# A hybrid decoder layer on one core: attention scores from split operands, x in three tiles that W_out fills, y split two tiles ahead, and other orders at two places

## The chip, the cores and the metric

The kernel runs on 1 core of one Trainium2 chip. The metric is the device time of one execution in microseconds (us). Engines are named as in the profile: PE (TensorE matmul), PEld (TensorE weight load), DVE (VectorE), ACT (ScalarE), POOL (GpSimd), SP (SyncE, which issues the DMAs).

## The reference, cut to what matters

One layer on 1024 tokens of width 1024, with 16 meta tokens ahead of them, so 1040 positions:

```
xn   = rms_norm(h)                                   # h: 1040 x 1024
z, xbc, dt, q, k, v = split(xn @ w_in)               # q, k, v: 16 heads of 64
y_ssd = ssd_mixer(z, xbc, dt, ...)                   # Mamba-2, chunks of 128
zlog = (q_t . k_s) / 8                               # per head
A[t,s] = sigmoid(zlog[t,s]) * prod_{s<j<t} (1 - sigmoid(zlog[t,j]))     # s < t
y_sb = rms_norm(A @ v)
h    = h + rms_norm([y_ssd ; y_sb] @ w_out)
g, u = split(rms_norm(h) @ w_up)                     # 2816 columns each
h    = h + rms_norm((gelu(causal_dwconv3(g)) * u) @ w_down)
```

Everything is float32, and the output is the last 1024 rows of h.

## The kernel before, in words

Large products are taken in float32r (F32R in the code, fp32r in the profile). An operand a is split into a_hi, its copy in float32r (an ACT copy), and a_lo = a - a_hi (a subtract on DVE or POOL), and a product is the sum of three matmuls, hi·hi + hi·lo + lo·hi, in one PSUM bank. Smaller products (scores, the mix with the values, transposes) are plain float32; the trace has two records for each such matmul of the scores.

**Projections.** The normed x stands transposed in two tiles, `xh` and `xl` (128 x 8 x 1040). `project_steps` (L154) makes 128 output columns of `w_in`: for each token third of `CH` (348, 346, 346 tokens) and each of 8 blocks of the contraction three matmuls (L162, `pj_*`), 24 in a third; ACT evacuates it. The projections for the attention are generators that other code advances by one step; a step is a third, or with `halves_` half a third (12 matmuls). They are the *fill* of the attention.

**Decays.** At 70 to 90 us the mixer's dt goes through a chain of small DVE operations (up to `s` and `adh`, L522 and L526), then `decays` (L531) multiplies it by three triangular matrices (`pz_ea`, `pz_de`, `pz_cd`) and ACT takes exponentials. Before it four steps of projections (`run(fill, 4)`) and the transposes of B (`bc[0][1][0]`, tiles `tt_B`) are issued.

**Attention.** A loop over 8 pairs of heads p and 8 query blocks i (L898). The order on PE is written out by hand (`manual_schedule`, L896): PE does what stands next in the code. For block i:

- `block_weights` (L682): scores `z` (L699) of 128 queries against n = 16 + 128(i+1) keys, in chunks of at most 512 keys (one chunk for i up to 2, two for i from 3 to 6, three for i = 7). The two heads of the pair lie on rows 0 to 63 and 64 to 127 of q and k. ACT makes two sigmoids of each chunk (`kp` L700, `bt` L701); DVE scans `kp` along the keys (L704) and POOL multiplies `bt` by it (L706), once per head.
- fill: one or two half steps of projections between the scores and what follows.
- `block_mix` (L725): `av` (L734), the product with the values, of the block whose transposes stand one block earlier.
- `block_turn` (L709): `tw` (L720), the transposes of `bt` of the block two earlier; ACT copies them to `th` (L722).
- one more half step of fill.

z and tw share two PSUM buffers ("zz"). In pair 6 the projections end; the x tiles are freed, and the first half of `w_out` is loaded, split into `woha`/`wola` (L827, L828) and multiplied with two halo rows (`halo`, L820), all behind blocks 5 and 6. From then on the fill is the first half of the output product, `ssd_half` (L876): for each token tile t, `split_y` loads `yk` and splits it into `yh` (ACT, L859) and `yl` (POOL, L860), and `out_steps` makes two halves of 24 matmuls (`mo`, L870). In pair 7 a half is placed only behind blocks 1, 3, 5, 6 and 7; `split_y` for tile t+1 stands ahead of the product of tile t.

**After the attention** the second half of `w_out` is loaded (`wor`, `worb`) and split, with its halo matmuls, while `ssd_half` ends with tiles 6 to 8. Then the second product runs tile by tile; `ev2` (L1322) adds it to the first, `after` (L1011 to L1024) takes the norms, `turn_x2` (L1030) transposes, and the feed-forward part begins with the products `g0a` and `u0a` (L1180). Their weights are split into `wh` (ACT, L1108) and `wl` (POOL, L1109). From t = 6 on the order on PE, DVE, ACT and POOL is that of the code (L1312).

Of the kernel before, what the change touches and what calls it, by code (L numbers as in the profile page):

```python
# [8 lines left out]
F32 = mybir.dt.float32  # L9
# [22 lines left out]
CH = [(0, 348), (348, 346), (694, 346)]  # L32
# [19 lines left out]
def tile_layer(ctx: ExitStack, tc: tile.TileContext, x, meta, rows, parts,  # L52
# [101 lines left out]
    def project_steps(w, ncol, xh, xl, chunks, evac, name, halves_=False):  # L154
        hi, lo = w
        for c0, n in chunks:
            acc = psum_mm(f"pj_{name}_{c0}")
            for k in range(KB):
                if halves_ and k == KB // 2:
                    yield  # L160
                for j, (a, b) in enumerate(((hi, xh), (hi, xl), (lo, xh))):
                    mm(acc[:ncol, :n], a[:, k, :ncol], b[:, k, c0:c0 + n],  # L162
                       start=(k == 0 and j == 0), stop=(k == KB - 1 and j == 2))
# [33 lines left out]
    xh = xp.tile([P, KB, L], F32R, name="xh", tag="xh")  # L197
    xl = xp.tile([P, KB, L], F32R, name="xl", tag="xl")

    def conv_chain(b, nm, w, halves_=False):  # L200
# [5 lines left out]

        return raw, project_steps(w, P, xh, xl, CH, ev, nm, halves_)

    dtT = rp.tile([32, L + 3], F32, name="dtT", tag="rt", bufs=1)

    def dt_steps(hl):
        for c0, n in CH:
            acc = psum_mm(f"pj_dt_{c0}")
            for k in range(KB):
                for j, src in enumerate((xh, xl)):
                    mm(acc[:32, :n], hl[:, k, :], src[:, k, c0:c0 + n],
                       start=(k == 0 and j == 0), stop=(k == KB - 1 and j == 1))
# [4 lines left out]
    with tc.tile_pool(name="pre", bufs=3, side="right") as pre, \  # L222
# [46 lines left out]
        def turn_x(i):  # L269
            c0, nr = spans[i]  # L270
            tps = []
            for hf in range(2):
# [6 lines left out]
                tps.append((tp, (slice(None), slice(4 * hf, 4 * hf + 4), slice(c0, c0 + nr))))  # L279
            for tp, dst in tps:  # L280
                nc.scalar.activation(xh[dst], tp[:, :, :nr], AF.Copy)
            for tp, dst in tps:
                nc.vector.tensor_tensor(xl[dst], tp[:, :, :nr], xh[dst].bitcast(F32), op=ALU.subtract)
# [62 lines left out]
    def qkv_block(name, evac, halves_):  # L346
        w = weights_of(name)
        for i, _ in enumerate(project_steps(w, P, xh, xl, CH, evac, name, halves_)):
# [3 lines left out]

    def qkv_steps(p, post):
        q = rp.tile([P, L + 3], F32, tag="rq", name=f"q{p}", bufs=3)
        k = rp.tile([P, L], F32, tag="rk", name=f"k{p}", bufs=3)
        for dst, nm in ((q, "q"), (k, "k")):
            def ev(acc, c0, n, dst=dst):
                nc.scalar.activation(dst[:, c0:c0 + n], acc[:, :n], AF.Copy)

            yield from qkv_block(f"{nm}{p}", ev, p > 1 or (p, nm) == (1, "k"))  # L360
        vt = rp.tile([P, L], F32, tag="rt", name=f"vt{p}", bufs=1)

        def evv(acc, c0, n):
            nc.scalar.activation(vt[:, c0:c0 + n], acc[:, :n], AF.Copy)

        v = rp.tile([P, NT + 1, P], F32, tag="rv", name=f"v{p}")
        vc = rp.tile([P, P], F32, tag="vc", name=f"vc{p}")
        heads[p] = q, k, v, vc
        yield from qkv_block(f"v{p}", evv, p > 0)

        def turn_v(part):
            tp = psum_tp(f"vtp{p}_{part}")
# [5 lines left out]
        def turn_edge():  # L378
            edge = rp.tile([P, NT, NM], F32, tag="edge", name=f"edge{p}", bufs=1)
# [7 lines left out]
            nc.vector.tensor_copy(meta_k[:, p, :], k[:, 0:NM])  # L387
# [20 lines left out]
    with tc.tile_pool(name="ssd", bufs=1, side="right") as sp:  # L408
# [49 lines left out]
        def z_steps(g, b):  # L458
# [5 lines left out]
            yield from project_steps(load_w(w_z[4 * g + b], P, f"z{g}{b}"), P, xh, xl, CH, evz, f"z{g}{b}")  # L464
# [75 lines left out]
        run(fill, 4)  # L540
        bc[0][1][0]()
        decays()
        tmp.close()
        run(fill)

# [135 lines left out]

    def block_weights(p, i):  # L682
        q, k = heads[p][:2]
        nm = f"{p}_{i}"
        if i == 0:
            edges[p] = ap.tile([P, 2, NT, NM], F32, tag="cb", name=f"cb{p}", bufs=2)
            nc.gpsimd.memset(edges[p][:, :, :, NM - 1:], 0.0)
        t0, n = NM + i * P, NM + (i + 1) * P
# [4 lines left out]
        for ci, (a, w) in enumerate(chunks):  # L693
# [3 lines left out]
            for j in range(2):  # L697
                h = halves[j]
                mm(z[:, j, :w], q[h, t0:t0 + P], k[h, a:a + w], start=True, stop=True)  # L699
            nc.scalar.activation(kp[:, :, a:a + w], z[:, :, :w], AF.Sigmoid, scale=-QSCALE)  # L700
            nc.scalar.activation(bt[:, :, a:a + w], z[:, :, :w], AF.Sigmoid, scale=QSCALE)  # L701
        m = n - NM
# [1041 lines left out]
```

## Time and profile before

| what | value |
|---|---|
| median of 3 runs | 1810.53 us (1805.03 to 1811.18) |
| the profiled execution | 1805.86 us |
| its span in the profile | 1804.2 us (1.66 us lie around it) |
| mean granted TensorE clock | 0.989 |
| busy | PE 1732.4 us (96%), PEld 1487.3, DVE 1061.6, ACT 830.8, POOL 867.8 |

Start of pairs: the first score of pair 0 is at 415.2 us and that of pair 7 at 880.5; the last scores are at 940.8. The page gives busy time by engine; the windows give it by stage; the timeline shows each instruction's start with the idle time ahead of it and what ended that. A line such as `L820` is a line of the kernel before.

### The profile page before, as it was taken

To read this page: it belongs to the slowest core of one execution; us is meant where nothing else is said; L and a number is where in the kernel's file an instruction comes from. 1 tells how busy PE (TensorE), PEld (TensorE's weight loads), DVE (VectorE), ACT (ScalarE), POOL (GpSimd) and SP (SyncE) were. 2 spreads that over 40 slices of the span, in tenths; PEclk is the share of its full clock that TensorE was granted. 3 is DMA by queue.
4 is the path that set the end of the run, shared out by engine and by line. 5 is a ranking of instruction groups with operands and counts; after the bars stand their busy time and mean duration, and the time that the engine had idled before them with its cause. 6 is when DMAs were issued, how large, how long until landed. Compare 5 with 4: busy or idle time off the path is not lost. (4 is left out here: it accounts for less than half of the span.)

```text
span 1804.2 us, 27314 instructions
## 1 busy us (share of the span) xinstructions
PE 1732.4 (96%) x10942; PEld 1487.3 (82%) x10942; DVE 1061.6 (59%) x1125; ACT 830.8 (46%) x1373; POOL 867.8 (48%) x615
## 2 busy tenths in 40 slices
PE   6999999999999999999799899899999999999997
PEld 6899889888888888886567588888999988888886
DVE  5651964873463454355741256666766666657988
ACT  5423553645565565566653333543333333244444
POOL 4223753676555564554751223277777776600001
PEclk9999999999999999999999899999999999999999
DMA  4133333231011011012212545222333332196344
GB/s 157 48 97 106 106 118 107 71 94 36 24 37 48 24 36 37 24 48 71 72 42 95 193 140 164 82 88 88 117 100 106 101 105 88 64 320 227 95 123 158
DMA packets 90547, 173.96 MB, mean 96 GB/s; under 512 B 10698, under 2 KB 35818, under 8 KB 90420
## 3 DMA queue, kind: packets, MB, share of 16 engines
q1 hardware_dynamic: 90420, 172.21, 30.0%
q8 instruction: 86, 1.41, 0.3%
q14 instruction: 41, 0.34, 0.1%
HBM read 122.39 MB, written 49.79 MB: 95 GB/s over the span
## 5 line engine op out<-in xcount | busy, mean ns | idle before, releaser
L704 DVE TENSOR_TENSOR_SCAN kp<-kp,hold 128x272 f32<-128x272 f32 (+7 forms) x128 | 207.8, 1665 | 193.5 <-ACT kp L700 103.2
L706 POOL TENSOR_TENSOR bt<-bt,kp 128x256 f32<-128x256 f32 (+7 forms) x128 | 214.7, 1695 | 188.9 <-DVE kp L704 132.7
L1109 POOL TENSOR_TENSOR wl<-wr,wh 128x1024 fp32r<-128x1024 f32 x44 | 110.7, 2524 | 40.7 <-ACT wh L1108 40.7
L1557 PE MATMUL dn<-dl,dh 128*128 128x512 f32 x308 | 119.9, 389 | 0.1
L1557 PE MATMUL dn<-dh 128*128 128x512 f32 x308 | 119.9, 389 | 0.0
L1557 PE MATMUL dn<-dh,dl 128*128 128x512 f32 x308 | 119.8, 389 | 0.0
L1603 POOL TENSOR_TENSOR fms<-fms,nhalf 128x1 f32<-128x1 f32 x8 | 8.5, 1060 | 225.7 <-DMA ar<-fda 186.0
L700 ACT ACTIVATE kp<-z 128x288 f32<-128x288 f32 (+6 forms) x112 | 82.8, 739 | 56.7 <-PE z L699 33.0
L1486 ACT ACTIVATE dh<-ar 128x512 fp32r<-128x512 f32 x77 | 48.7, 632 | 111.3 <-PE dn L1557 90.7
L699 PE MATMUL z<-k,q 64*128 64x144 f32 (+6 forms) x448 | 86.9, 487 | 13.3 <-ACT bt L701 6.0
L1108 ACT ACTIVATE wh<-wr 128x1024 fp32r<-128x1024 f32 x44 | 46.6, 1060 | 114.7 <-PE fX L1166 68.3
L1238 DVE SCALAR_TENSOR_TENSOR ga<-gr,pp,ga 128x1024 f32<-128x1024 f32 x44 | 71.4, 1622 | 34.8 <-ACT ga L1231 34.0
L722 ACT ACTIVATE th<-tw 128x1024 f32<-128x1024 f32 (+2 forms) x96 | 74.7, 813 | 34.1 <-PE tw L720 32.2
L701 ACT ACTIVATE bt<-z 128x288 f32<-128x288 f32 (+6 forms) x112 | 83.1, 742 | 0.0
L720 PE MATMUL tw<-ident,bt 128*128 128x128 f32 x576 | 77.6, 280 | 3.8 <-issue 2.8
L734 PEld LDWEIGHTS av<-th,v 128*64 128x64 f32 x1152 | 62.6, 138 | 18.9 <-issue 17.9
L734 PE MATMUL av<-th,v 128*64 128x128 f32 x1152 | 78.0, 281 | 0.0
L1487 DVE TENSOR_TENSOR dl<-ar,dh 128x512 fp32r<-128x512 f32 x77 | 53.2, 691 | 41.7 <-ACT dh L1486 41.7
L720 PEld LDWEIGHTS tw<-ident,bt 128*128 128x128 f32 x576 | 62.1, 141 | 15.5 <-issue 12.9
L699 PEld LDWEIGHTS z<-k,q 64*128 64x128 f32 x448 | 36.7, 186 | 41.8 <-issue 18.5
L1557 PEld LDWEIGHTS dn<-dl,dh 128*128 128x128 f32 x308 | 57.8, 188 | 12.5 <-DVE dl L1487 0.4
L1557 PEld LDWEIGHTS dn<-dh 128*128 128x128 f32 x308 | 57.8, 188 | 12.4 <-ACT dh L1486 0.3
(550 smaller groups left out, 5752.6 us busy)
## 6 DMA issues: line engine op xcount, KB each, us to landing
wr<-in_w_up SPq DMA_DIRECT2D x44, 512.0 KB
fds<-ga SPq DMA_DIRECT2D x44, 256.0 KB
b<-in_w_down SPq DMA_DIRECT2D x44, 256.0 KB
ar<-fds SPq DMA_DIRECT2D x44, 256.0 KB
fda<-ga SPq DMA_DIRECT2D x33, 256.0 KB
ar<-fda SPq DMA_DIRECT2D x33, 256.0 KB
yk<-yd SPq DMA_DIRECT2D x16, 512.0 KB
zd<-zt SPq DMA_DIRECT2D x8, 520.0 KB
```

The lines of the kernel that those rows point to most:

```text
L699: mm(z[:, j, :w], q[h, t0:t0 + P], k[h, a:a + w], start=True, stop=True)
L700: nc.scalar.activation(kp[:, :, a:a + w], z[:, :, :w], AF.Sigmoid, scale=-QSCALE)
L701: nc.scalar.activation(bt[:, :, a:a + w], z[:, :, :w], AF.Sigmoid, scale=QSCALE)
L704: nc.vector.tensor_tensor_scan(kp[:, j][:, ::-1], kp[:, j][:, ::-1], hold[:, L - n:L][:, ::-1], 0.0, op0=ALU.mult, op1=ALU.max)
L706: nc.gpsimd.tensor_tensor(bt[:, j, 0:m], bt[:, j, 0:m], kp[:, j, 1:m + 1], op=ALU.mult)
L720: nc.tensor.transpose(tw[:, j, b, :], bt[:, j, c0:c0 + P], ident)
L722: nc.scalar.activation(th[:, :, :nb, :], tw[:, :, :nb, :], AF.Copy)
L734: mm(av[halves[j], :], v[:, kb, halves[j]], th[:, j, b, :], start=kb == 0, stop=kb == i)
L1109: nc.gpsimd.tensor_tensor(l, raw, h.bitcast(F32), op=ALU.subtract)
L1238: nc.vector.scalar_tensor_tensor(v, self.g[jj][:, :, i:i + 256], fconv_w[:, j, i:i + 1], v, op0=ALU.mult, op1=ALU.add)
L1487: sub(lo[:, k], raw, hi[:, k].bitcast(F32), op=ALU.subtract)
L1557: mm(banks[t], u[:, 0, c], v[:, 1, :], start=(p == 0 and i == 0), stop=(p == NPR - 1 and i == 2))
```

## The change

1. **Scores.** `k` is kept as two float32r tiles, `kh` (ACT copy) and `kl` (DVE subtract from PSUM). `split_q` makes `qh` (DVE cast, 128 x 128) and `ql` (DVE subtract) for a block. A chunk of scores is three float32r matmuls for each head, in place of one float32 matmul. `split_q` of the next block stands behind this block's sigmoids.
2. **Order in the attention.** `block_mix` stands right behind the first two chunks of scores, ahead of the fill. The fill has a table: `FILL` blocks of each pair get a second half step ahead of the transposes. The projections of pair 7 go by token thirds (q, k, v of one third, then of the next).
3. **x by thirds.** `xh`, `xl` become three tiles of 400, 384 and 256 tokens, each with both halves. When a third has been used for the last time, its tile takes pieces of the split `w_out` (`third_slots`), one or two a block from pair 6, block 2, to pair 7, block 1. `ssd_half` then advances half a tile behind each further block.
4. **y two tiles ahead.** `split_y` is called for tile t+2.
5. **Decays.** `run(fill, 5)` ahead of `decays`, and the transposes of B behind the fill.
6. **Way into the feed-forward part.** For the last tile `run(steps)` (with `ev2`) stands ahead of the last steps of `turn_x2`; `run(norm, 1)` moves behind the first product of `g0a`; `u0a` is started ahead of `turn_x2(8)`.

```diff
-CH = [(0, 348), (348, 346), (694, 346)]
+CH = [(0, 400), (400, 384), (784, 256)]
...
-            for j in range(2):
-                h = halves[j]
-                mm(z[:, j, :w], q[h, t0:t0 + P], k[h, a:a + w], start=True, stop=True)
+            for s_, (u, r) in enumerate(((qh, kh), (ql, kh), (qh, kl))):
+                for h, j in zip(halves, range(2)):
+                    mm(z[:, j, :w], u[h, :], r[h, a:a + w], start=s_ == 0, stop=s_ == 2)
...
+    def split_q(p, i):
+        q = heads[p][0][:, NM + i * P:NM + (i + 1) * P]
+        qh = rp.tile([P, P], F32R, tag="qh", name=f"qh{p}_{i}", bufs=2)
+        ql = rp.tile([P, P], F32R, tag="ql", name=f"ql{p}_{i}", bufs=2)
+        nc.vector.tensor_copy(qh, q)
+        nc.vector.tensor_tensor(ql, q, qh.bitcast(F32), op=ALU.subtract)
+        qsplit[p, i] = qh, ql
...
+            nc.scalar.activation(kh[:, c0:c0 + n], acc[:, :n], AF.Copy)
+            nc.vector.tensor_tensor(kl[:, c0:c0 + n], acc[:, :n], kh[:, c0:c0 + n].bitcast(F32), op=ALU.subtract)
...
+    FILL = (3, 2, 1, 1, 1, 1, 1, 0)
+    STAGE = {(6, 2): 1, (6, 3): 2, (6, 4): 3, (6, 5): 4, (6, 6): 5, (6, 7): 6, (7, 0): 7, (7, 1): 8}
...
             next(block, None)
+            if mix:
+                block_mix(*mix.pop(0))
...
-            run(fill, 1 + (i < 3))
+            run(fill, 1 + (i < FILL[p]))
             run(block)
-            if mix:
-                block_mix(*mix.pop(0))
...
+            for _ in range(2):
+                if wsteps and len(wres) < min(8, 3 * left[0], STAGE.get((p, i), 0)):
+                    run(wsteps, 1)
...
-            run(first, int(p == 7 and (i % 2 or i > 5) or p == 6 and i == 7))
+            elif first:
+                run(first, 1)
...
-            if t < NT:
-                ys.append(split_y(wp, 0, t + 1, ("whi", "wlo", WB)))
             y = ys.pop(0)
+            if t < NT - 1:
+                ys.append(split_y(wp, 0, t + 2, ("whi", "wlo", WB)))
...
-        run(fill, 4)
-        bc[0][1][0]()
+        run(fill, 5)
         decays()
         tmp.close()
         run(fill)
+        bc[0][1][0]()
...
             run(norm)
+            if t == NT:
+                run(steps)
             run(turn)
...
     norm = after(8, mt, P, xt, None, junk)
-    run(norm, 1)
...
     run(ga_, 1)
-    run(norm, 1)
+    run(norm, 2)
...
-    turn8 = turn_x2(8, P, xn8, x2_tiles(8))
-    run(turn8, 1)
...
     run(ua_, 1)
+    turn8 = turn_x2(8, P, xn8, x2_tiles(8))
+    run(turn8, 1)
```

What the change moves, at three places. First, PE in a block of the attention with i = 5 (pair 1; before; `z_5_0` and `z_5_1` are its two chunks of scores, `pj_v_694` is fill, `av_2` the mix of block 2, `tw_3` the transposes of block 3):

```order
L699 MATMUL z_5_0_4916<-k_3827,q_3826 128x392 x2
L699 MATMUL z_5_1_4921<-k_3827,q_3826 128x392 x2
L162 MATMUL pj_v_694_4901<-xh,wh_v_4637 128x346
L162 MATMUL pj_v_694_4901<-xl,wh_v_4637 128x346
L162 MATMUL pj_v_694_4901<-xh,wl_v_4638 128x346
...
L734 MATMUL av_2_4944<-th_2_0_4899,v_4144 64x128 x6
L720 MATMUL tw_3_0_4952<-ident,bt_3_4790 128x128 x8
```

The same place on PE now:

```order
L748 MATMUL z_5_0_5054<-kh_3830,qh_5_5002 128x392 x2
L748 MATMUL z_5_0_5054<-kh_3830,ql_5_5003 128x392 x2
L748 MATMUL z_5_0_5054<-kl_4077,qh_5_5002 128x392 x2
L748 MATMUL z_5_1_5063<-kh_3830,qh_5_5002 128x392 x2
L748 MATMUL z_5_1_5063<-kh_3830,ql_5_5003 128x392 x2
L748 MATMUL z_5_1_5063<-kl_4077,qh_5_5002 128x392 x2
L786 MATMUL av_2_5081<-th_2_0_5037,v_4507 64x128 x6
L162 MATMUL pj_v_784_5089<-xs_136,wh_v_4772 128x256 x2
L162 MATMUL pj_v_784_5089<-xs_136,wl_v_4773 128x256
...
L772 MATMUL tw_3_0_5102<-ident,bt_3_4903 128x128 x8
```

Two rows of scores have become six, and the mix has moved from behind the fill to right behind the scores. Second, the DMAs that SP issues at the end of the attention (`wor`, `worb` are pieces of the second half of `w_out`, `yk_t` the load of tile t of y; `yk_1` there belongs to the second product). Before:

```order
L807 DMA worb_9073<-in_w_out 128x1024
L807 DMA worb_9075<-in_w_out 128x1024
L807 DMA worb_9077<-in_w_out 128x1024
L807 DMA wor_9079<-in_w_out 128x1024
L807 DMA wor_9081<-in_w_out 128x1024
L807 DMA worb_9083<-in_w_out 128x1024
L858 DMA yk_1_9089<-yd_101 128x1024
L858 DMA yk_7_9095<-yd_99 128x1024
L886 DMA mixd_108<-ma_9101 128x512 x2
```

And now, from the load of tile 7 on:

```order
L924 DMA yk_7_9703<-yd_99 128x1024
L952 DMA mixd_105<-ma_9433 128x512 x2
L859 DMA wor_9795<-in_w_out 128x1024
L952 DMA mixd_106<-ma_9592 128x512 x2
L859 DMA wor_9797<-in_w_out 128x1024
...
L859 DMA worb_9809<-in_w_out 128x1024
L924 DMA yk_1_9815<-yd_101 128x1024
L924 DMA yk_8_9821<-yd_100 128x1024
```

`yk_7` has moved ahead of all eight pieces of `w_out`; the last of them is followed by `yk_8`. Third, ACT on the way into the feed-forward part (`gr_0` is the copy of the first product out of PSUM, `t4l` the square sum of the last tile, whose input `mb` is what `ev2` writes). Before:

```order
L1047 ACTIVATE b22s<-x2tp_10172 128x4x128
L1054 ACTIVATE xb<-x2tp_10172 128x4x128
L1108 ACTIVATE wh_10188<-wr_10049 128x1024
L1011 ACTIVATE t4l,oss_10239<-mb_10140 128x1024
L1186 ACTIVATE gr_0_10245<-g0a_10246 128x516
```

Now:

```order
L1112 ACTIVATE b22s<-x2tp_10892 128x4x128
L1119 ACTIVATE xb<-x2tp_10892 128x4x128
L1173 ACTIVATE wh_10934<-wr_10769 128x1024
L1251 ACTIVATE gr_0_10959<-g0a_10960 128x516
L1076 ACTIVATE t4l,oss_10986<-mb_10860 128x1024
```

The copy of the product and the square sum have changed places.

More of the change, by code (lines that the diff above doesn't have):

```diff
@@ L351, in qkv_block @@
             yield
+    left = [0]
     def qkv_steps(p, post):
         q = rp.tile([P, L + 3], F32, tag="rq", name=f"q{p}", bufs=3)
[L355 to L361, printed above, removed]
```

130 lines of the change are left out of this document (87 added, 43 removed).

## Prediction

> **What bounds the kernel now.** I read the page first: busy time, then the slices.
>
> ```profile
> span 1804.2 us, 27314 instructions
> ...
> PE 1732.4 (96%) x10942; PEld 1487.3 (82%) x10942; DVE 1061.6 (59%) x1125; ACT 830.8 (46%) x1373; POOL 867.8 (48%) x615
> ```
>
> PE is busy for 96% of the span and no other compute engine for 60%, so PE is the bound. Time can be won in two ways only: less work on PE, or some of PE's 72 us of idle time. The windows tell where that lies.
>
> ```profile
> 50.00:130.00 80.00, 76.27 (x478) 73.86 (x477) 51.03 (x60) 32.20 (x52) 18.66 (x14) 0.96 0.24 67
> 603.90:672.00 68.10, 67.81 (x518) 57.22 (x517) 30.66 (x24) 39.49 (x66) 38.86 (x30) 1.00 0.13 34
> 838.00:940.00 102.00, 83.19 (x581) 56.74 (x581) 64.09 (x43) 66.90 (x109) 72.71 (x48) 0.97 0.22 69
> 985.00:1011.00 26.00, 18.13 (x77) 10.35 (x77) 10.24 (x10) 14.86 (x17) 7.39 (x4) 0.80 0.72 244
> 1119.00:1156.00 37.00, 30.58 (x186) 27.41 (x185) 27.57 (x33) 15.83 (x27) 9.27 (x7) 0.95 0.31 100
> 1156.00:1804.00 648.00, 636.84 (x3609) 556.54 (x3608) 459.67 (x521) 250.60 (x356) 309.97 (x169) 1.00 0.39 126
> ```
>
> A row is a stretch, its length, the busy time of PE, PEld, DVE, ACT and POOL, the granted clock, then DMA. Pair 3 of the attention (second row) fills PE, 67.81 of 68.10 us: there only less work helps. The end of the attention (third) idles for 18.8 us, the stage behind it (fourth) for 7.9 at a clock of 0.80, the way into the feed-forward part (fifth) for 6.4. The last 648 us aren't touched.
>
> **Scores.** This is PE in block 7 of pair 3 (start, length, line, operation, count):
>
> ```profile
> 662.86 0.32 PE L162 MATMUL pj_q<-xh,wl_q 128*128 128x346 f32 x1
> 663.11 1.44 PE L699 MATMUL z<-k,q 64*128 64x348 f32 x8
> 664.48 0.43 PE L162 MATMUL pj_q<-xh,wh_q 128*128 128x346 f32 x1
> 664.75 0.32 PE L162 MATMUL pj_q<-xl,wh_q 128*128 128x346 f32 x1
> ...
> 666.33 0.32 PE L162 MATMUL pj_q<-xh,wl_q 128*128 128x346 f32 x1
> 666.58 0.85 PE L699 MATMUL z<-k,q 64*128 64x344 f32 x4
> 667.36 1.31 PE L734 MATMUL av<-th,v 128*64 128x128 f32 x20
> ```
>
> From start to start the scores take 1.37 us (two chunks) and 0.78 us (one), 2.15 us for 1040 keys of both heads. A float32r matmul of 346 columns follows the last one after 0.158 us (664.75 to 666.33 are ten). At each change of kind about 0.1 us is lost: 0.25 us from 662.86 to 663.11 and 0.27 from 664.48 to 664.75, where 0.16 would do. If the two heads of a float32r product run side by side, as those eight float32 records do in 1.37 us, three chunks take 9 x 0.158 = 1.42 us, with 0.4 us for the ends of two bursts 1.82: 0.33 us less. A pair has 4736 keys in its eight blocks, 4.55 times 1040: 1.5 us, in eight pairs **-12 us**. No row shows float32r on 64 rows. At best a quarter of 2.15 us goes, 0.54 us or -20 in all; at worst the heads run one after the other, and nine more slots make it 1.42 x 4.55 x 8 = 52 us worse than I take. I take side by side: the nearest row, z itself, has it on the same halves.
>
> **Changes of kind.** Before, a block goes fill, scores, fill, mix, transposes, fill, and four of these borders are between full and half width, 0.1 us each; now fill, scores, mix, fill, transposes, fill has three. In 7 of 8 blocks (block 7 has a third chunk apart) that is 56 x 0.1, about **-5 us**, between -6 and 0.
>
> **Fill at the end of the attention.**
>
> ```profile
> L162 PE MATMUL pj_v<-xl,wh_v x192: 315/321/332, 371.3 to 836.4; 128*128 128x346 f32 x128, 128*128 128x348 f32 x64
> ```
> ```profile
> 867.56 1.52 PE L699 MATMUL z<-k,q 64*128 64x344 f32 x4 [4.71 <-ACT bt L701]
> 875.06 0.50 PE L870 MATMUL mo<-woha,yl 128*128 128x512 f32 x1 [2.24 <-POOL yl L860]
> ...
> 901.21 1.08 PE L699 MATMUL z<-k,q 64*128 64x264 f32 x4 [2.29 <-DVE thc L746]
> ```
>
> The projections are used up at 836.4, in block 3 of pair 6, since each pair takes 19 half steps (two a block and three more) and the 18 of the next pair don't last. Behind that PE waits for the attention's own chain (brackets: idle time, releaser): 18.8 us of idle, and 0.03 of 102 us in clock, 3 us. With `FILL` a pair takes 17 (16 in pair 0, 18 in pair 1), so that the projections reach pair 7, and the halo products and halves of `mo` are spread over what follows. The same work then fills the gaps. I keep 6 to 8 us of waits, since a dozen of these gaps are of 0.4 to 1 us and stand within a block: **-14 us**; between -5 and -19.
>
> What could eat this: ACT in block 7 must evacuate six sigmoids, two `th` and a projection, and pair 3 has ACT busy for 39.49 of 68.1 us; PE's pair falls to 68.1 - 1.5 - 0.7 - 2 x 1.9 = 62 us, so ACT is still at 64%.
>
> **Splits on DVE.** New are a cast and a subtract (128 x 128) a block, and three subtracts of kl from PSUM a pair.
>
> ```profile
> L283 DVE TENSOR_TENSOR xl<-xtp,xh 128x512 fp32r<-128x512 f32 x12 | 7.7, 677 | 0.0
> ...
> L526 DVE CAST adh<-s 128x144 fp32r<-128x144 f32 x1 | 0.2, 235 | 0.0
> ```
> ```profile
> 76.22 0.31 DVE L527 TENSOR_TENSOR adl<-s,adh 128x144 fp32r<-128x144 f32 x1
> ```
> ```profile
> L704 DVE TENSOR_TENSOR_SCAN kp<-kp,hold 128x1040 f32<-128x1040 f32 x12 | 28.8, 2444 | 21.8 <-issue 20.8 <-ACT kp L700 1.0
> ...
> L704 DVE TENSOR_TENSOR_SCAN kp<-kp,hold 128x144 f32<-128x144 f32 x14 | 23.1, 1690 | 2.2 <-ACT kp L700 2.2
> L386 DVE COPY meta_q<-q 64x2 f32<-64x2 f32 x12 | 17.0, 1419 | 0.6 <-ACT q L358 0.5
> ...
> L704 DVE TENSOR_TENSOR_SCAN kp<-kp,hold 128x272 f32<-128x272 f32 x14 | 9.5, 717 | 28.1 <-ACT kp L700 28.0
> ```
>
> By the cast of 235 ns, the subtract of 0.31 us and the 677 ns from PSUM, that is 8 x 0.54 + 3 x 0.68 = 6.4 us a pair; if cast and subtract are each held up as the 64x2 copy is (1.42 us), 8 x 2.84 + 2 = 25 us. Either way DVE, with its 30.66, has at most 56 of 62 us, so I cost it at nothing: the scans have it covered as long as a split is done before its block's scores. The split stands a block ahead, behind the previous block's sigmoids; queued behind it on DVE is that block's scan, and POOL's multiply and, two blocks later, `tw` wait for that. If the cover went, 0.4 us in each of 56 blocks would be +22.
>
> The scan rows also bear on who shares what. The scan of 144 columns takes 1690 ns where 272 columns take 717, so DVE is held up at times; yet from 272 to 1040 columns it grows by only 2.25 ns a column, though the second scan of a block runs while POOL multiplies the first head. The Trainium skill, "SBUF — State Buffer", section "Who interferes with whom", has a rule that speaks against this change: a DVE instruction with two SBUF inputs and a GpSimd instruction that reads SBUF exclude each other for their whole length. By that rule in full the sum would be that of the third rival below, by the rows it stays as it is; the short scans speak for it, the long ones against.
>
> **y two tiles ahead.**
>
> ```profile
> 998.24 1.03 PE L820 MATMUL halo<-worb,y 128*2 128x512 f32 x4 [1.87 <-DMA worb<-in_w_out]
> 1003.15 1.22 PE L870 MATMUL mo<-woha,yh 128*128 128x512 f32 x2 [3.88 <-ACT yh L859]
> 1006.47 0.80 PE L870 MATMUL mo<-woha,yl 128*128 128x512 f32 x1 [2.10 <-POOL yl L860]
> ```
> ```profile
> 975.33 0.39 PE L870 MATMUL mo<-wola,yh 128*128 128x512 f32 x1
> ...
> 976.48 0.39 PE L870 MATMUL mo<-woha,yl 128*128 128x512 f32 x1
> ```
> ```profile
> 994.49 0.33 SPq L807 DMA_DIRECT2D worb<-in_w_out  x1
> 994.87 0.90 SPq L858 DMA_DIRECT2D yk<-yd  x2
> ```
>
> Tile 7 of y is issued only behind the last piece of `w_out`, at 994.87, and PE waits 1.87 + 3.88 + 2.10 = 7.9 us in a stretch with the clock at 0.80, which takes 5 us more from 26. Now tile 7 is split long before, and its 48 matmuls stand among the halo pieces; while they run, 48 x 0.23 = 11 us (975.33 to 976.48 are five), tile 8 is loaded and split, which took tile 7 from 994.87 to 1006.47. A microsecond or two of waits stays: **-12 us**, between -8 and -14.
>
> **Decays and feed-forward entrance.**
>
> ```profile
> 75.97 0.21 PE L534 MATMUL pz_ea<-s,tri 16*16 16x16 f32 x2 [0.85 <-DVE s L522]
> 80.20 1.11 PE L431 MATMUL tt_B<-ident,bt 128*128 128x128 f32 x4 [2.88 <-DVE bn L427]
> ```
> ```profile
> 1137.08 0.58 PE L1180 MATMUL g0a<-b21h,wh 128*128 128x258 f32 x1 [4.53 <-ACT gr L1186]
> 1146.14 1.06 PE L1030 MATMUL x2tp<-ident,oxn 128*128 128x128 f32 x8 [1.60 <-DVE oxn L1024]
> ```
> ```profile
> 1141.17 1.06 ACT L1108 ACTIVATE wh<-wr 128x1024 fp32r<-128x1024 f32 x1
> ...
> 1142.52 2.39 POOL L1109 TENSOR_TENSOR wl<-wr,wh 128x1024 fp32r<-128x1024 f32 x1
> ```
>
> At the decays 3.7 us of idle and 0.04 of 80 us in clock (3 us) are at stake. The wait for `bn` goes, but `pz_cd` now waits for the exponentials, which stand behind more work on ACT; **-2 us**, between -5 and +2. At the entrance the 4.5 us go, since the copy `gr` no longer stands behind the square sum. Late next is `u0a`, now ahead of the transposes: its `wh` ends at 1142.2 and its `wl` at 1144.9, a few us earlier once the chain ahead of them is, while PE would reach it near 1138 (1137.08 - 4.53, and the 7.5 us that it now runs from 1137.08 to its next gap, less 1.9 us that the clock of 0.95 takes from 37). So most of the gap moves, 4 us or so: **-2 us**, between -6 and +2. The other thirds of x have the same 1040 columns and the same matmuls: 0.
>
> **Sum.** 1805.86 - 12 - 5 - 14 - 12 - 2 - 2 = 1758.9, so **1759 us**. The profiled execution is near the low end of the three runs (1805.03 to 1811.18, median 1810.53); up to 5 us more can come from that.
>
> **Rivals.**
> - *The splits delay the scans.* DVE held up by POOL at each split, 0.4 us a block on PE: 1759 + 22 = 1781. For it the short scan and the copy of 1419 ns, against it DVE's slack. 0.15.
> - *The heads run one after the other in float32r*: 1759 + 52 = 1811, no change. Against it z's own side by side; for it only that no row shows it. 0.06.
> - *DVE and POOL take turns*, the slower side. In pair 3 they are busy for 30.66 + 38.86 us, with the splits 75.9; in turn that is 13.9 us over PE's 62, and in the six pairs from 1 to 6 gives 1759 + 83 = 1842. It is slower than before once the two overlap by less than some 6 us in a pair. Before, 69.5 us of the two fit into 68.1, which it would need almost wholly in turn; but the long scans show no wait. 0.06. (The rule of the Trainium skill, "SBUF — State Buffer", is this rival's.)
> - *It does not do what it says*: the idle time only moves (to `u0a`, `pz_cd`, `tw` and tile 8), and only the saved work, 17 us, comes: 1789. 0.09.
>
> **How the numbers follow.** My forecast has 0.64, with 1742 to 1776 by its terms' ends. The range, 1741 to 1794, takes in the first and the last rival. A measurement of this kernel tells 0.5%, 9 us, from no change: faster than 1797 has 0.64 + 0.15 + 0.09, with a little taken off for what I haven't seen: 0.86; within it 0.07; slower 0.07.
>
> **What would show it.** Scores: in block 7 near 1.15 us from the first z to `av`, with starts of two heads some 7 ns apart; 0.3 us between each would be the second rival. Pairs 1 to 5 with a period of 62 us, against 68.1. PE idle for under 8 us from the last projections to the last scores, and the first score of pair 7 near 851. No idle time over 2 us between the attention and tile 8, clock near 1. A wait of 3 to 5 us at `u0a`. The prediction is wrong if a pair's period stays over 65 us, or if a stage with the clock at half speed stands where none was.

## The result and the profile after

| | before | after |
|---|---|---|
| median | 1810.16 us (4 runs, 1805.03 to 1811.18) | 1774.83 us (4 runs, 1772.30 to 1777.55) |
| ratio, 95% interval | | 0.9818 [0.9801, 0.9835] |
| profiled execution, its span | 1805.86, 1804.2 us | 1777.14, 1775.4 us |

The kernel is 1.8% faster. The forecast of 1759 us was 16 us too low; the measured time lies inside its range, 1741 to 1794. Each experiment below but the last is a single run, and the four runs of the changed kernel alone differ by 5 us, so the parts are read from stages of the traces and not from total times. The page first:

```profile
span 1775.4 us, 27924 instructions
...
PE 1715.6 (97%) x11166; PEld 1507.1 (85%) x11166; DVE 1123.2 (63%) x1277; ACT 824.3 (46%) x1371; POOL 868.9 (49%) x615
```

PE is busy for 17 us less (1732.4 before), the 12 + 5 that the forecast took off its work, and is still the bound. The windows of the changed kernel (same columns as before): pair 3, pair 6, pair 7 up to the last score, the stretch behind it, the second output product, the way into the feed-forward part, the rest.

```profile
591.20:654.00 62.80, 61.29 (x518) 55.02 (x517) 40.43 (x42) 37.51 (x63) 36.85 (x30) 1.00 0.12 35
778.90:851.70 72.80, 66.94 (x544) 58.01 (x543) 47.84 (x50) 42.26 (x68) 37.37 (x28) 0.98 0.14 44
851.70:923.00 71.30, 63.05 (x481) 50.42 (x477) 35.59 (x38) 40.62 (x71) 44.05 (x35) 0.95 0.29 94
923.00:1011.00 88.00, 86.77 (x479) 67.21 (x476) 18.86 (x21) 33.02 (x46) 23.12 (x10) 0.98 0.45 147
1011.00:1100.60 89.60, 87.28 (x412) 71.98 (x411) 54.87 (x73) 34.10 (x60) 27.81 (x22) 1.00 0.46 153
1100.60:1154.00 53.40, 49.61 (x303) 44.18 (x303) 35.29 (x36) 26.63 (x36) 20.81 (x13) 0.94 0.26 85
1154.00:1775.00 621.00, 609.82 (x3448) 532.86 (x3446) 443.64 (x510) 237.73 (x345) 295.51 (x161) 1.00 0.39 128
```

In pairs 6 and 7 PE is idle for 5.9 + 8.3 us and loses some 5 us more by the clock of 0.98 and 0.95 (1.5 and 3.6 us of 72.8 and 71.3). That is where the forecast went wrong. Marks on PE, read from the starts of instructions in the timelines, give the same by stage:

| stage, us | before | after | change | forecast |
|---|---|---|---|---|
| start to first score | 415.2 | 412.5 | -2.7 | -2 |
| first score of pair 0 to that of pair 6 | 392.9 | 366.4 | -26.5 | -31 for this row |
| first score of pair 6 to the last score | 132.7 | 144.0 | **+11.4** | and this (scores, order, fill) |
| last score to tile 8 of the first output product | 78.2 | 66.3 | -11.9 | -12 |
| from there to the end of the second output product | 109.4 | 111.4 | +2.0 | 0 |
| from there to `fA`, the first product behind `g0a` and `u0a` and their like | 55.3 | 54.1 | -1.2 | -2 |
| the rest | 620.5 | 620.7 | +0.2 | 0 |

### The profile page after: what moved, and what is told of

Its sections match the earlier page's. It is cut to its first block, busy times and chain, and to the rows that moved or that the text cites. A ratio compares the mean times of both kernels' runs of the same rounds, so it can differ in the third digit from the quotient of the medians.

```text
span 1775.4 us, 27924 instructions
## 1 busy us (share of the span) xinstructions
PE 1715.6 (97%) x11166; PEld 1507.1 (85%) x11166; DVE 1123.2 (63%) x1277; ACT 824.3 (46%) x1371; POOL 868.9 (49%) x615
## 5 line engine op out<-in xcount | busy, mean ns | idle before, releaser
L756 DVE TENSOR_TENSOR_SCAN kp<-kp,hold 128x272 f32<-128x272 f32 (+7 forms) x128 | 185.5, 1490 | 29.9 <-ACT kp L749 22.4
L1552 ACT ACTIVATE dh<-ar 128x512 fp32r<-128x512 f32 x77 | 48.7, 632 | 111.4 <-PE dn L1623 87.9
L162 PE MATMUL pj_v<-xs,wh_v 128*128 128x400 f32 (+2 forms) x384 | 96.2, 338 | 3.8 <-DVE kl L382 3.8
L162 PE MATMUL pj_k<-xs,wh_k 128*128 128x400 f32 (+2 forms) x384 | 94.7, 334 | 0.8 <-ACT q L375 0.7
L162 PE MATMUL pj_q<-xs,wh_q 128*128 128x400 f32 (+2 forms) x384 | 95.4, 335 | 0.0
L724 DVE CAST qh<-q 128x128 fp32r<-128x128 f32 x64 | 38.5, 603 | 87.9 <-PE z L748 87.6
L1303 DVE SCALAR_TENSOR_TENSOR ga<-gr,pp,ga 128x1024 f32<-128x1024 f32 x44 | 71.3, 1621 | 34.8 <-ACT ga L1296 34.0
L162 PE MATMUL pj_X<-xs,wh_X 128*128 128x400 f32 (+2 forms) x384 | 92.7, 329 | 0.2 <-ACT craw_X L208 0.2
L162 PE MATMUL pj_z<-xs,wh_z 128*128 128x400 f32 (+2 forms) x384 | 92.2, 328 | 0.0
L936 PE MATMUL mo<-woa,yh 128*128 128x512 f32 x256 | 84.5, 403 | 1.6 <-ACT yh L925 1.6
```

The source lines that it names most:

```text
L162: mm(acc[:ncol, :n], a[:, k, :ncol], xs[c0][:, b, k, :n], start=(k == 0 and j == 0), stop=(k == KB - 1 and j == 2))
L756: nc.vector.tensor_tensor_scan(kp[:, j][:, ::-1], kp[:, j][:, ::-1], hold[:, L - n:L][:, ::-1], 0.0, op0=ALU.mult, op1=ALU.max)
L936: mm(acc, u[:, k, :], v[:, cs], start=(k == 0 and j == 0), stop=(k == 7 and j == 2))
L1303: nc.vector.scalar_tensor_tensor(v, self.g[jj][:, :, i:i + 256], fconv_w[:, j, i:i + 1], v, op0=ALU.mult, op1=ALU.add)
```

## The scores, and what each microsecond of them is worth

PE in block 7 of pair 3, changed kernel (start, length, operation; x2 are the two heads):

```profile
643.76 0.43 PE L748 MATMUL z<-kh,qh 64*128 64x348 f32 x2
644.03 0.33 PE L748 MATMUL z<-kh,ql 64*128 64x348 f32 x2
...
644.67 0.33 PE L748 MATMUL z<-kl,qh 64*128 64x348 f32 x2
644.92 1.31 PE L786 MATMUL av<-th,v 128*64 128x128 f32 x20
```

The two heads do run side by side (the two of a row start 1 to 7 ns apart), 0.16 us a product, and the first two chunks take 1.16 us from the first `z` to `av`: the forecast had 1.15, and 1.37 was before. With the third chunk it is 1.83 us, where the forecast had 1.82.

**Scores in float32 again.** All else as changed:

```diff
-            for s_, (u, r) in enumerate(((qh, kh), (ql, kh), (qh, kl))):
-                for h, j in zip(halves, range(2)):
-                    mm(z[:, j, :w], u[h, :], r[h, a:a + w], start=s_ == 0, stop=s_ == 2)
+            for h, j in zip(halves, range(2)):
+                mm(z[:, j, :w], q[h, t0:t0 + P], k[h, a:a + w], start=True, stop=True)
...
```

> The changed kernel with the scores as before: one float32 matmul per head and chunk, k kept in float32, no splits of q and k; all else as changed. Theory (the three float32r products save 0.33 us in block 7, 1.5 us a pair, and the splits on DVE are covered): pairs 2 to 5 start every 64 us instead of 62.1 to 62.8, the profiled time is 12 us longer, near 1789 against 1777. Rival (the splits on DVE, held up by POOL, cost what the products save): the period moves by under 0.4 us and the time by under 4.

1774.92 us, as fast as with the split scores. Yet both theories missed: pairs 2 to 5 start every 63.4 to 63.5 us (62.1 to 62.8 changed), a microsecond longer. On the mean of pairs 3 and 4, PE's time on z is 10.2 us a pair here and 8.8 in the changed kernel: the work fell by 1.4 us, as worked out, but the idle time of those pairs is 1.0 us here and 1.4 there. And pair 6 takes 69.4 us here against 72.8. From the first score to the last the split scores bring 2.9 us (513.3 to 510.4), of some 11 us of work (8 x 1.4): 6.4 us up to pair 6, of which pair 6 gives 3.4 back.

**The mix behind the fill.** `block_mix` back to its old place, all else as changed.

```diff
-            if mix:
-                block_mix(*mix.pop(0))
             if p > 0 and i == 3:
                 edge_mix(p - 1, edge)
             run(fill, 1 + (i < FILL[p]))
             run(block)
+            if mix:
+                block_mix(*mix.pop(0))
```

> The changed kernel with the mix back behind the fill, as before. Theory (four borders between half and full width a block cost 0.1 us each, three now): pairs 2 to 5 start every 63.3 us against 62.1 to 62.8. Rival (the place of the mix decides which wait ends last, above all the 0.84 to 0.88 us waits for the edges' copy at block 3 and for the sigmoids): the period moves by over 1 us, up or down.

1782.80 us. Pairs 2 to 5 start every 62.6, 62.7, 62.8 and 63.1 us, 0.3 us above the changed kernel on the mean: the sign of the theory, less than half its size. In pair 4 PE does 1.0 us more work than in the changed kernel (fill 35.0 against 34.5, transposes 7.9 against 7.5, the mix 0.1) and idles for 0.7 us where that idles for 1.3. Again the work went as forecast and part of it came back as waits: in the changed kernel `tw` waits 0.45 to 0.88 us for ACT's sigmoids in block 7 of each pair, and here not at all, or 0.28 us in pair 4.

**No thirds.** Parts 1, 4, 5, 6 and the place of the mix in the kernel before, with x, fill and W_out as before. Against the changed kernel:

```diff
-CH = [(0, 400), (400, 384), (784, 256)]
+CH = [(0, 348), (348, 346), (694, 346)]
...
-    FILL = (3, 2, 1, 1, 1, 1, 1, 0)
...
-            run(fill, 1 + (i < FILL[p]))
+            run(fill, 1 + (i < 3))
...
```

> The kernel before with the split scores, the new place of the mix, y two tiles ahead, the decays and the way into the feed-forward part, but x, the fill and W_out as before (parts 1, 4, 5, 6 and half of 2). Theory (thirds and the new fill took away 22 us of idle time and clock at the end of the attention, but new waits of about that length stand in pairs 6 and 7): as fast as the changed kernel within 6 us, 1771 to 1783, with a period of 66 us in pairs 1 to 5 and some 18 us of idle time from pair 6 on. Rival (the forecast: the thirds bring 14 us): 1791.

1794.72 us: my theory, made after the result, fell, and the forecast's term is nearer; the thirds and the new fill bring 17.6 us (to the 1777.14 us of the profiled execution). The windows of this kernel (pair 3, pair 6, pair 7) show why:

```profile
603.50:670.20 66.70, 65.41 (x546) 59.52 (x545) 41.59 (x43) 39.29 (x66) 39.76 (x30) 1.00 0.13 34
802.60:877.60 75.00, 59.96 (x482) 48.28 (x481) 57.11 (x49) 47.25 (x76) 42.78 (x29) 0.93 0.19 64
877.60:940.10 62.50, 55.83 (x425) 44.33 (x424) 28.62 (x33) 32.05 (x54) 36.44 (x33) 0.92 0.17 57
```

Pairs 1 to 5 are 1.8 us shorter each than before, but pairs 6 and 7 then idle for 21.7 us at clocks of 0.93 and 0.92: 137.5 us to the last score against 132.7 before. From first to last score it is 522.7 us, 3 us less than before, of the 9 that pairs 1 to 5 saved. So work that goes from PE in the attention is worth little while the projections end in pair 6, since most of what it saves is waited for at the end; the fill is what turns it into time.

## What is waited for in pairs 6 and 7

The two long waits of the changed kernel, with what stands ahead of them. Pair 6, block 4:

```profile
819.82 0.47 ACT L381 ACTIVATE kh<-pj_k 128x384 fp32r<-128x384 f32 x1
820.66 2.28 DVE L879 SCALAR_TENSOR_TENSOR woa<-wor,pp,woa 128x1024 fp32r<-128x1024 f32 x1
822.86 0.55 DVE L382 TENSOR_TENSOR kl<-pj_k,kh 128x384 fp32r<-128x384 f32 x1
823.46 1.01 PE L162 MATMUL pj_v<-xs,wh_v 128*128 128x384 f32 x2 [3.80 <-DVE kl L382]
```

ACT copied `kh` out of PSUM by 820.3, but the buffer is free only when DVE has taken `kl`, and DVE does a piece of W_out first. Pair 7, block 2:

```profile
861.25 1.59 DVE L879 SCALAR_TENSOR_TENSOR woa<-wor,pp,woa 128x1024 fp32r<-128x1024 f32 x1
863.54 0.33 SPq L924 DMA_DIRECT2D yk<-yd  x1
867.01 1.06 ACT L925 ACTIVATE yh<-yk 128x1024 fp32r<-128x1024 f32 x1
868.12 0.50 PE L936 MATMUL mo<-woa,yh 128*128 128x512 f32 x1 [1.60 <-ACT yh L925]
869.60 4.67 POOL L926 TENSOR_TENSOR yl<-yk,yh 128x1024 fp32r<-128x1024 f32 x2
871.99 0.79 PE L936 MATMUL mo<-woa,yl 128*128 128x512 f32 x1 [3.37 <-POOL yl L926]
```

The load of y's first tile is issued when the last raw pieces of W_out are split (862.84), since both take the same two raw tiles; the fill that is to hide it is that tile's own product.

**One piece of W_out later.**

```diff
-    STAGE = {(6, 2): 1, (6, 3): 2, (6, 4): 3, (6, 5): 4, (6, 6): 5, (6, 7): 6, (7, 0): 7, (7, 1): 8}
+    STAGE = {(6, 2): 1, (6, 3): 2, (6, 4): 2, (6, 5): 4, (6, 6): 5, (6, 7): 6, (7, 0): 7, (7, 1): 8}
```

> The changed kernel with one piece of W_out moved from pair 6, block 4, to block 5 (STAGE of (6, 4) is 2). Theory (the 3.8 us wait at 823 is for the subtract of kl, which stands on DVE behind the subtract of that piece; the wait brings 3.4 us of half clock, 1.7 us lost): both go, the last scores come 5 us earlier, 1772 against 1777. Rival (the halo sums hold one of the two PSUM buffers of the projections from pair 6, block 2, on, so that each third waits for the one before it): a wait of 2 us or more comes back at another third in pair 6, and the time stays within 2 us.

1776.14 us, and the wait is there unchanged (3.80 us, at 823.87). But the run tells nothing of the theory: in this part of the program only PE's order is that of the code, and the piece stood on ACT and DVE ahead of `kl` as it had (on DVE from 821.08, `kl` from 823.27).

**kl from a copy in SBUF**, in pair 7:

```diff
             nc.scalar.activation(kh[:, c0:c0 + n], acc[:, :n], AF.Copy)
-            nc.vector.tensor_tensor(kl[:, c0:c0 + n], acc[:, :n], kh[:, c0:c0 + n].bitcast(F32), op=ALU.subtract)
+            k32 = acc[:, :n]
+            if p == 7:
+                if c0 == 0:
+                    later["k32"] = rp.tile([P, L + 3], F32, tag="rq", name="k32", bufs=3)
+                k32 = later["k32"][:, c0:c0 + n]
+                nc.scalar.activation(k32, acc[:, :n], AF.Copy)
+            nc.vector.tensor_tensor(kl[:, c0:c0 + n], k32, kh[:, c0:c0 + n].bitcast(F32), op=ALU.subtract)
```

> The changed kernel, but in pair 7 ACT copies a third of k a second time, in float32, into a free tile, and DVE takes kl from that tile and not from PSUM (three ACT copies more, some 0.47 us each). Theory (the 3.8 us wait in block 4 of pair 6 comes because the projections' PSUM buffer is given back by DVE, which does a piece of W_out first): PE waits under 1 us there, no half clock there, the first score of pair 7 comes 68 us after that of pair 6 and not 72.8. Rival (the buffer isn't it; pair 6 is short of work that is ready): a wait of about 3 us at the same fill or the next one, 72 to 73 us.

```profile
820.99 0.48 ACT L387 ACTIVATE k<-pj_k 128x384 f32<-128x384 f32 x1
821.52 0.30 PEld L162 LDWEIGHTS pj_v<-xs,wh_v 128*128 128x128 f32 x2 [1.20 <-ACT k L387]
821.53 0.62 PE L162 MATMUL pj_v<-xs,wh_v 128*128 128x384 f32 x2 [0.96 <-ACT k L387]
```

1773.43 us. The wait is 0.96 us and for ACT, no half clock stands there, and pair 7 starts 68.5 us after pair 6, 4.3 us sooner: the theory holds.

**No halo sums**, the halo products of the first half left out and their sum set to zero:

```diff
-                halo = psum_mm("halo0")
-                wsteps = wout_steps(third_slots(), 0, ssd_g, wres, halo_y(ap, 0, ssd_g), halo, [])
+                wsteps = wout_steps(third_slots(), 0, ssd_g, wres, halo_y(ap, 0, ssd_g), None, [])
...
```

> The changed kernel without the halo products of the first half of W_out (the sums are set to zero), so that no halo sum holds one of the two PSUM buffers of the projections in pairs 6 and 7, and 4 x 0.97 us of PE work are left out. Theory (the wait of 3.8 us needs both: DVE giving the buffer back late, and the halo sum holding the other one): the wait goes, and the first score of pair 7 comes 4 (halo) + 5.5 us sooner after that of pair 6, 65 to 66 us against 72.8 less what of the halo falls into pair 7, 64 to 68. Rival (the wait is for DVE alone): it stays, 70 to 71 us.

1765.18 us with that work missing; pair 6 takes 66.8 us, and no wait for `kl` is left, though DVE still takes it. So the wait needs both: DVE giving one PSUM buffer back late, and the halo sum, which the spread over eight blocks has made hold the other for some 50 us. The first theory had named only one half of the cause.

**y early**: tiles 1 and 2 get raw tiles of their own and are split at pair 7, block 0.

```diff
...
-                ys1 = [split_y(wp, 0, t, ("whi", "wlo", WB)) for t in (1, 2)]
...
+            if p == 7 and i == 0:
+                ys1 = [split_y(wp, 0, t, ("whi", "wlo", WB),
+                               rp.tile([P, L + 3 if t == 1 else L], F32, tag=tg, name=f"yr{t}", bufs=3)[:, :D].rearrange("p (a b) -> p a b", b=P))
+                       for t, tg in ((1, "rq"), (2, "rk"))]
```

> The changed kernel with tiles 1 and 2 of y loaded into free tiles of their own and split at pair 7, block 0, instead of behind the last piece of W_out. Theory (the 1.6 and 3.4 us waits at 868 and 872 are for the load and split of y, queued behind the raw pieces of W_out, and bring 6.8 us of half clock, 3.4 lost): they go, the first score of block 3 of pair 7 comes 8 us earlier (872 against 880.4), 1769 against 1777. Rival (ACT, DVE and POOL are crowded in pair 7, and the waits only move): the last scores come under 3 us earlier than 920, with new waits in blocks 3 to 6.

1769.02 us as forecast. Pair 7 from its first score to its last is 63.0 us against 71.2, with no wait at the first `mo`. But pair 6 got 3.4 us longer (76.2), which I hadn't expected: 1.6 us of it is more idle time, 1.7 a half-clock stretch at 848.6. With both waits taken away at once:

> The changed kernel with both waits taken away: tiles 1 and 2 of y early in tiles of their own, and kl of pair 7 from a copy in SBUF. Theory (two causes that do not touch each other): 8.4 + 4.3 us less from the first score of pair 6 to the last, less some 3 us that the early splits gave back between pairs 6 and 7; the last score 136 us after the first of pair 6, against 144.0, 1765. Rival (pair 7 is short of work anyway): no better than 1769.

1765.98 us; the last score comes 133.9 us after the first of pair 6. Part of what was given back shows in this run at the end of pair 6. `tw` takes one of the two PSUM buffers that it shares with the scores, which is free when ACT has made the second sigmoid (`bt`) of them, and ACT does the split `yh` of the second tile first:

```profile
843.04 1.15 ACT L931 ACTIVATE yh<-yr 128x1024 fp32r<-128x1024 f32 x1
...
845.15 0.85 ACT L756 ACTIVATE bt<-z 128x688 f32<-128x688 f32 x1
...
846.05 0.66 PE L778 MATMUL tw<-ident,bt 128*128 128x128 f32 x4 [1.24 <-ACT bt L756]
```

> As the run with both waits taken away, but tile 2 of y split at pair 7, block 2, and only tile 1 at block 0. Theory (the early splits gave 3 us back because two yl on POOL stand ahead of the multiply of block 7 and two yh on ACT ahead of its sigmoids): 1.5 us better than with both at block 0, 1763 to 1764. Rival (the give-back comes from the projections' order): no difference over 0.5 us between the first score of pair 6 and the last.

1766.66 us. (In this run the products of tiles 2 and 3 of y are exchanged.) From the first score of pair 6 to the last it takes 131.7 us, 2.2 us less, but only 0.6 us of that is idle time: `tw` waits 0.45 us there and not 1.24. The other 1.7 us is a half-clock stretch at 900.6 that only the run before it had, behind gaps of 0.3 us. So the second tile stood in the way for about half a microsecond, just over what the rival allowed; the total doesn't show it, as half-clock stretches elsewhere fell otherwise. The last run keeps `kl` from SBUF, and takes tile 1 of y early and tile 2 as in the changed kernel:

```diff
...
+            if p == 7 and i == 0:
+                ys1.append(split_y(wp, 0, 1, ("whi", "wlo", WB),
+                                   rp.tile([P, L + 3], F32, tag="rq", name="yr1", bufs=3)[:, :D].rearrange("p (a b) -> p a b", b=P)))
...
-                ys1 = [split_y(wp, 0, t, ("whi", "wlo", WB)) for t in (1, 2)]
+                ys1.append(split_y(wp, 0, 2, ("whi", "wlo", WB)))
```

> The changed kernel with kl of pair 7 taken from a copy in SBUF, tile 1 of y loaded early into a tile of its own and split at pair 7, block 0, tile 2 as in the changed kernel. Theory (the two waits explain most of what the forecast had too much, and only tile 1 is waited for): the last score 132 to 134 us after the first of pair 6 (144.0 in the changed kernel), no half clock between 815 and 890, a median near 1764, ratio to before near 0.976. Rival (tile 2 then comes late, behind the last piece of W_out): a wait of 1 us or more at block 4 of pair 7, and 1768 or more.

**1763.45 us** in the median (1761.55 to 1764.75, 5 runs), 0.9755 [0.9741, 0.9769] of before. Its windows over pair 6, pair 7 and a little more:

```profile
778.90:851.70 72.80, 69.78 (x594) 60.48 (x593) 53.28 (x52) 45.09 (x76) 41.85 (x29) 1.00 0.20 63
851.70:925.00 73.30, 69.13 (x521) 55.54 (x519) 35.80 (x40) 45.62 (x77) 48.64 (x38) 1.00 0.24 78
```

131.6 us to the last score, and the clock is 1.00 in both. Its two edits bring 11.4 us between the medians, of the 16 us by which the forecast was too low. Whether the split scores bring more of their 11 us of work here than in the changed kernel was not run.

## y, the decays, the way in, and the splits

**Three parts as before** (y one tile ahead, decays, way into the feed-forward part), each read at its own place:

```diff
-            y = ys.pop(0)
-            if t < NT - 1:
-                ys.append(split_y(wp, 0, t + 2, ("whi", "wlo", WB)))
+            if t < NT:
+                ys.append(split_y(wp, 0, t + 1, ("whi", "wlo", WB)))
+            y = ys.pop(0)
...
-        run(fill, 5)
+        run(fill, 4)
+        bc[0][1][0]()
         decays()
...
```

> The changed kernel with three parts as before: y one tile ahead, the decays, the way into the feed-forward part; each is read from its own stage. y: tile 8 of the first output product starts 78 us after the last score, against 66.3 (12 us, as forecast; rival: the other order of the halo pieces alone does it, under 4 us). Decays: the first score of pair 0 comes 2 to 3 us later than the 409.4 to 412.5 of the changed kernel (rival: it lies within that spread). Way in: from the end of the second output product to the first of the feed-forward products 55.3 us as before against 54.1 (rival: no difference, 0.3 or less).

1786.58 us. PE behind the attention, and at the way in:

```profile
978.29 1.03 PE L872 MATMUL halo<-worb,y 128*2 128x512 f32 x4 [1.89 <-DMA worb<-in_w_out]
983.36 1.22 PE L936 MATMUL mo<-woa,yh 128*128 128x512 f32 x2 [4.04 <-ACT yh L925]
986.47 0.80 PE L936 MATMUL mo<-woa,yl 128*128 128x512 f32 x1 [1.89 <-POOL yl L926]
```
```profile
1117.47 0.45 PE L1245 MATMUL g0a<-b21h,wh 128*128 128x258 f32 x1 [4.53 <-ACT gr L1251]
1126.54 1.06 PE L1095 MATMUL x2tp<-ident,oxn 128*128 128x128 f32 x8 [1.54 <-DVE oxn L1089]
```

The three waits of before are back, and tile 8 starts 77.8 us after the last score: y two ahead is worth 11.5 us. The way in takes 55.3 us as before; with the new order the gaps are these two, in the changed kernel:

```profile
1112.54 0.50 PE L1245 MATMUL u0a<-b11h,wh 128*128 128x512 f32 x1 [1.86 <-ACT wh L1173]
1115.21 0.80 PE L1245 MATMUL u0a<-b11h,wl 128*128 128x512 f32 x1 [1.94 <-POOL wl L1174]
```

As forecast, most of the gap moved to `u0a`; 1 to 2 us are won (53.2 to 54.3 us in the kernels with the new order). The decays can't be told: the first score comes at 412.3 us with the old order, and between 409.9 and 414.0 with the new one in kernels that are alike up to there.

**Splits three times**:

```diff
-        nc.vector.tensor_copy(qh, q)
-        nc.vector.tensor_tensor(ql, q, qh.bitcast(F32), op=ALU.subtract)
+        for _ in range(3):
+            nc.vector.tensor_copy(qh, q)
+            nc.vector.tensor_tensor(ql, q, qh.bitcast(F32), op=ALU.subtract)
```

> The changed kernel with every cast and subtract of split_q done three times (the same values): 16 DVE instructions more a pair and kind, 8 to 19 us more on DVE, whose pair goes from 38 us busy to 47 to 57 of 62. Theory (the splits are covered, and POOL and DVE do not take turns as a rule): the period of pairs 2 to 5 stays at 62.1 to 62.8, at most 0.5 us longer; the time within 4 us of 1777. Rival (DVE is already the one that ends last where PE waits 0.84 to 0.88 us, at the edges' copy in block 3): the period grows by 1 us or more, and the wait at block 3 with it. Rival (DVE and POOL take turns): a period of 70 us or more.

1783.08 us. A stretch of one period across pairs 3 and 4 (pair 4 starts at 657.2), and the first product of v that waits:

```profile
654.00:716.30 62.30, 61.51 (x519) 55.45 (x519) 53.83 (x74) 37.50 (x64) 37.79 (x30) 1.00 0.12 35
```
```profile
828.20 1.01 PE L162 MATMUL pj_v<-xs,wh_v 128*128 128x384 f32 x2 [5.34 <-DVE kl L382]
```

With DVE busy for 53.83 and POOL for 37.79 of 62.30 us, the period is the same (62.1, 62.7, 62.3, 62.6): the splits are covered. That the two busy times add up to more than the period does not show that the engines never take turns, since an instruction that is held up counts as busy; the last section shows that they do. The wait at block 3 stays at 0.84 to 0.89 us in pairs 3, 5 and 6, so the length of the splits isn't its cause. The 6 us that the time grew by lie in pair 0 (56.5 us against 52.3, with a half-clock stretch of 6.8 us at 428.9 that costs 3.4 of it; other kernels with one split have 52 to 54) and at the two waits of pairs 6 and 7, which grew by 1.5 us each.

## Why the prediction was right, and where it was not

The direction and the range were right, and so were the stages behind the attention. The attention, from the first score to the last, gave 15.2 us (525.6 to 510.4) of the 31 that were forecast for it.

- *Scores, -12*: the work was sized rightly (1.83 us in block 7, 1.4 us a pair), side by side as taken. As time it brought 6.4 us up to pair 6 and 2.9 us up to the last score, the rest coming back as waits, above all that for `kl`.
- *Changes of kind, -5*: a microsecond of work a pair, and 0.3 us in the period. With the mix behind the fill the stretch from the first score to the last is 4.5 us longer (514.9 to 510.4), of which 1.7 is a half-clock stretch at 431.8.
- *Fill, -14*: **the step that failed**. "The same work then fills the gaps. I keep 6 to 8 us of waits." Pairs 6 and 7 kept 14 us of idle time and 5 of clock (19.4 and 3.4 before). I had asked what the fill takes away and not what the fill itself must wait for: the spread halo sum holds a PSUM buffer, DVE gives the other back behind W_out, and y's first tile waits for W_out's raw tiles. Taking the two waits away gives 1763 us; the thirds with the new fill are worth more than I said (17.6 us), since without them the first two terms are waited away too. The three terms don't add up one by one.
- *Splits on DVE, 0*: right within 0.6 us a pair up to pair 5. In pair 6 it was not the splits of q that were waited for but `kl`, which I priced at 0.68 us and hid without asking who waits for its PSUM buffer.
- *y, -12*: 11.9 from before to after, 11.5 by the undone part. *Way in, -2*: 1 to 2. *Decays, -2*: open.
- *Not foreseen*: +2.0 us in the second output product. 1.7 us of it is a half-clock stretch at 1004; in the kernels without one there (float32 scores, 109.9 us; the last kernel, 110.1; both waits taken away, 110.5) it is 0.5 to 1.1. *Pairs 1 to 5* idle 0.8 to 1.5 us each against 0.3, 4.3 us more in all. 0.37 to 0.86 of it is z waiting for DVE at block 3 (the masked copy of the edges, L798, or `meta_k`); with float32 scores that wait is 0.29 us in these pairs, as before, so it grew with the split scores, by which step was not tried. The rest is above all `tw` in block 7, which the mix behind the fill took away.
- Of the rivals, none came true alone. The first (POOL holds DVE up at each split) gave 1781 and is nearest in time, but three times the splits left the period as it was. The last (the idle time only moves) is nearest in kind, though it moved to `kl` and to y and not to the places named. The third (DVE and POOL take turns) had the mechanism and not the price: the busy times that it added up already hold the waiting. The prediction took the long scans, which kept their time, as a sign against it; they had started first, and it was POOL's multiply that was held up (last section).
- *Signs.* The pairs' period (62.1 to 62.8, pair 1 64.3), the first score of pair 7 (851.7), the quiet stretch up to tile 8 (no gap over 0.5 us) and the waits at `u0a` (1.86 + 1.94) came as said. PE idles for 8.3 us from the last projection, at 855.1, to the last scores, near the 8 that were said; the sign missed the wait for `kl`, which stands before it. Two signs of being wrong came too, both in pairs 6 and 7: pair 6 took 72.8 us (72.4 before), over the 65 that were named, and a stretch at half clock stands at 823.3, where none was.
- *Its bounds.* The 1742 to 1776 given for the terms' ends is not their sum: added up, the ends give 1736 to 1785, without the rival of heads one after the other.

## What to carry to other kernels

Work taken from the bound engine becomes time only where other work stands ready at the end of the stage: look first at what the last part of a pipelined loop waits for. When filler work is spread out, list the buffers it holds for longer (PSUM sums, raw tiles) and what the filler itself waits for; a filler that must be loaded needs its load ahead of, and not behind, the work that it follows. A PSUM buffer that two engines read is free only when the later of them is done, and that one may have other work in its queue first. When you add up busy times of two engines, ask whether time in which one waits for the other is counted in them.

## What the runs showed of the hardware

Float32r matmuls of two heads on 64 rows each start 1 to 7 ns apart in that block and take 0.16 us for 348 columns, the pitch of one matmul of 346 columns on 128 rows.

A change between full and half width costs about 0.1 us here too: in that block 0.21 us lie between the last matmul of `pj_v` (256 columns, 0.12 us apart) and the first of the scores.

DVE and POOL hold each other up. These are the end of pair 6 and block 0 of pair 7 in the changed kernel:

```profile
850.93 2.30 DVE L756 TENSOR_TENSOR_SCAN kp<-kp,hold 128x1040 f32<-128x1040 f32 x1
851.19 3.84 POOL L758 TENSOR_TENSOR bt<-bt,kp 128x1024 f32<-128x1024 f32 x1 [3.10 <-DVE kp L756]
853.15 1.96 DVE L724 CAST qh<-q 128x128 fp32r<-128x128 f32 x1
...
854.99 1.99 POOL L758 TENSOR_TENSOR bt<-bt,kp 128x1024 f32<-128x1024 f32 x1
855.14 1.99 DVE L725 TENSOR_TENSOR ql<-q,qh 128x128 fp32r<-128x128 f32 x1
```

The second head's scan starts first and takes its usual 2.30 us. The multiply of the first head starts 0.25 us later and takes 3.84 us, where the same multiply with no scan beside it takes 1.99: it is longer by about the time that the scan still ran. The cast, 0.23 us in the median, then lasts until that multiply ends (855.11 and 855.02), and the subtract, 0.29 us in the median, until the second one ends (857.13 and 856.98). A scan that starts behind a multiply is held up in the same way: one of 912 columns at 451.91 took 4.20 us where others take 2.03. So whichever starts first keeps its time, and the other waits about as long as they overlap. The rule of the Trainium skill, "SBUF — State Buffer", section "Who interferes with whom", that a DVE instruction with two SBUF inputs and a GpSimd instruction that reads SBUF exclude each other, fits the scans and the subtract; the cast, with one SBUF input, was held up as well. Three times the splits left the period of pairs 2 to 5 as it was, so there this cost PE next to nothing.

Waits of 3.8 us, and of 1.6 and 3.4 us close together, each had a stretch at half clock with them (3.4 and 6.8 us long, from 823.3 and 871.1). Such a stretch costs half its length, so that 5 us of waits cost 8.4. But stretches of 3.4 us also came where PE had waited for no more than 0.41 us in the 12 us ahead (from 1004.3 in the changed kernel, from 900.6 with both waits taken away), so these traces give no threshold. In the stretch before the attention they fell otherwise from run to run, 4 us between kernels that are the same there.
